# Decoder trunk, 288 tokens: norm sums as products with ones, pooling by doubling additions, first loads in pairs

## The chip, the cores and the metric

The kernel runs on one core of a Trainium2 chip. The metric is the device time of one execution in microseconds (us), the median of several runs, each against the same kernel before on the same chip. Less is better.

## The reference

One layer of a decoder trunk over 288 tokens: 256 of a new prompt and 8 x 4 new tokens of running requests, width 2048. All is float32. Cut to what matters:

```python
def trunk_layer(x, hist_conv, hist_pool, pos0, ...):
    h = rmsnorm(x, norm1_g)
    proj = einsum("btd,de->bte", h, w_in) + b_in          # 2048 -> 3 x 1024
    a, gate, z = proj[..., :1024], proj[..., 1024:2048], proj[..., 2048:]
    u_ext = concatenate([hist_conv, a * sigmoid(gate)], axis=1)
    c = silu(layernorm(depthwise_causal_conv(u_ext, conv_w, conv_b), ln_g, ln_b))   # 31 taps
    z_ext = concatenate([hist_pool, z], axis=1)
    d = multiscale_pool(z_ext, pos0)     # 4 groups of 256 channels: mean of the last 2, 4, 8, 16 tokens, minus z
    p = einsum("btgc,gce->btge", d, pool_w).reshape(bsz, T, 1024) * pool_scale
    x = x + einsum("btm,md->btd", concatenate([c, p], axis=-1), w_out)
    h2 = rmsnorm(x, norm2_g)
    x = x + einsum("btf,fd->btd", square(relu(einsum("btd,df->btf", h2, w_ff1))), w_ff2)   # 2048 -> 8192 -> 2048
```

A final rmsnorm follows, and the last conv and pool inputs are outputs as well. rmsnorm divides by the root of the mean square over the channels of a token (plus 1e-6); layernorm subtracts the mean first.

## The kernel before

**Layout.** Channels lie on the 128 partitions and the 288 tokens on the free axis, so xT is 128 x 16 x 288 in SBUF. A sum over the channels of a token thus runs across partitions, and TensorE has to do it.

**Products.** Float32 accuracy comes from three products in fp32r: a value is split in a high part (a cast on ScalarE) and a low part (value minus high part). `product` (L297) issues hi·hi (L300), hi·lo (L301) and lo·hi (L302), each 128x128 by 128x288. Weights are streamed by SP's queue into tiles `wr` (128x1024, six buffers) and split by `split` (L288) in `whi` on ScalarE (L293) and `wlo` on VectorE or GpSimd (L294), four buffers of each. An accumulator is a PSUM bank `ac` (four) or `cv` (two); two more banks `ms` hold sums.

**Stages**, in the order of the program:
1. A first loop over eight pairs of x blocks, c = 0 to 7 (L367-405), gives conv groups 0 and 1. For each block it makes hh and hl, x times the norm gain, split (L376, L377), and splits the weight (L383, L384). Steps c = 0 and 1 work on halves. `square(c)` (L357) squares the pair on ScalarE (128x576) and adds it up on VectorE; the 1/rms itself (`rb`, L404) is applied to the results of the products.
2. Conv groups 2 to 6, the pool groups 3, 2, 1, 0 and conv 7, in the order of SEQUENCE (L46), the pool mixes between. A conv group multiplies its two banks by rb (L416, L417), gates them, and runs 31 taps on VectorE and GpSimd (`conv_taps`, L443, L436).
3. w_out, pool half: 8 groups of 48 matmuls (L548-556). While they run, the conv layernorm is prepared: `norm_begin` (after the third group) subtracts the mean over channels and sums the squares in `ssc`, `norm_end` (after the fifth) forms the root and the eight pairs mh, ml of normed, SiLU'd channels.
4. w_out, conv half: 8 groups whose right-hand sides are those mh, ml (L560).
5. Four chunks of ff1 and ff2, and the final norm (L687).

**Sums before.** Per-token sums of squares come from `token_sum` (L232): three matmuls, with 96 tokens as the stationary operand and a column of ones, give 96x3 in PSUM. `rsqrt_rows` (L266) makes the reciprocal root of these 96x3 numbers: sqrt on ScalarE, then on VectorE one Newton-like step in five small instructions with two reciprocals (L275-279). Then three matmuls with an identity (L285, `pr`) spread them over all partitions as 128x288. For the conv norm's mean one float32 matmul with `avg` (ones/1024) is used (L521). Only the norm ahead of ff1 uses the wide way: `column_sum` (L244), two fp32r matmuls with a 128x128 of ones on the split squares, and `rsqrt_wide` (L249), the same step on 128x288.

**Pooling before.** `pool_group` (z with 15 tokens of history, L457-480) sums w = 2, 4, 8 or 16 neighbours by `tensor_reduce` on VectorE over overlapping windows; for w = 16 in two levels (L467-472).

**What sets the order.** The Tile scheduler puts all instructions in one order per engine, from the program's priorities and its own timeline. Each engine runs its row strictly in that order; a later instruction cannot pass a waiting one. The order below is that of the compiled program.

Of the kernel before, what the change touches and what calls it, by code (L numbers as in the profile page):

```python
# [88 lines left out]
def trunk_kernel(ctx: ExitStack, tc: tile.TileContext, io):  # L89
# [33 lines left out]
    def act(name, **kw):  # L123
        return slot(name, F32R, **(kw or {"tag": "act"}))
# [4 lines left out]
    def ms(name, n=512):  # L129
        return msp.tile([P, n], F32, name=nm(name), tag="ms", padded_shape=[P, 512])  # L130
# [7 lines left out]
    def f32(t):  # L138
        return t[:].bitcast(F32)
# [34 lines left out]
    def load_x(k, n):  # L174

        nc.sync.dma_start(xT[:, k : k + n, :], io["xT"][:, k : k + n, :])
# [6 lines left out]
        nc.sync.dma_start(to[:, :, k0:k1, :], src[:, :, at + k0 : at + k1, :])  # L183

    nc.scalar.dma_start(vec[:, 0:CWO], io["vec"][:, 0:CWO])
    load_x(0, 1)
    load_first(0, 0, 1)
    load_x(1, 1)
    load_first(0, 1, 2)
    load_x(2, 2)  # L190
    load_first(1, 0, 1)
    load_first(1, 1, 2)
    load_x(4, 2)
    load_first(2)
    load_x(6, 4)
    load_first(3)
    load_x(10, 4)
    load_first(4)
    load_x(14, 2)
    load_first(5)  # L200
    nc.sync.dma_start(vec[:, CWO:NV], io["vec"][:, CWO:NV])
    load_first(6)
# [2 lines left out]

    ones = const.tile([P, P], F32, name="ones")
    nc.vector.memset(ones, 1.0)
    avg = const.tile([P, P], F32, name="avg")
    nc.vector.memset(avg, 1.0 / DC)
    ones_r = const.tile([P, P], F32R, name="ones_r")  # L210
    nc.vector.memset(ones_r[:].bitcast(F32), 1.0)
    few = const.tile([P, 1], F32, name="few")
# [21 lines left out]
        for j in range(3):  # L234
            nc.tensor.matmul(pt[:TB, j : j + 1], t[:, j * TB : (j + 1) * TB], ones[:, 0:1], start=first and j == 0, stop=last and j == 2)  # L235

    def parts(t):

        th, tl = (tmpp.tile([P, T], F32R, name=nm(n), tag="tmp", bufs=6) for n in ("th", "tl"))
        nc.gpsimd.tensor_copy(th, t)  # L240
        nc.gpsimd.tensor_tensor(tl, t, f32(th), op=ALU.subtract)
        return th, tl

    def column_sum(bank, by, hilo):  # L244
# [1 line left out]
        for j, t in enumerate(hilo):  # L246
            nc.tensor.matmul(bank[:, :T], by, t, start=j == 0, stop=j == 1)

    def rsqrt_wide(bank, out, scale):  # L249

        s1, s2 = tmp("s"), tmp("s")
        b = bank[:, :T]
        nc.scalar.activation(s1, b, AF.Sqrt, bias=eps[:, 0:1], scale=scale)
        nc.vector.tensor_scalar(b, b, scale / 2, EPS / 2, op0=ALU.mult, op1=ALU.add)
        nc.vector.reciprocal(s2, s1)
        nc.vector.tensor_tensor(b, b, s2, op=ALU.mult)
        nc.vector.scalar_tensor_tensor(out=s2, in0=s1, scalar=0.5, in1=b, op0=ALU.mult, op1=ALU.add)
        nc.vector.reciprocal(out, s2)
# [93 lines left out]

    hx = []
    first_banks = bank2() + [bank("cv", cvp, "cv") for _ in range(2)]
    total = ms("total", 8)

    def square(c):  # L357

        to = squares[:, 0] if c == 0 else squares[:, 1 + c % 3]
        nc.scalar.activation(to, xT[:, 2 * c : 2 * c + 2, :], AF.Square)  # L360
# [6 lines left out]
    for c in range(8):  # L367
        pair = []
        hi = wspl.tile([P, 4, 256], F32R, name=nm("whi"), tag="whi")
        lo = wspl.tile([P, 4, 256], F32R, name=nm("wlo"), tag="wlo")  # L370
        views = [t[:].rearrange("p (b k) n -> p b k n", b=2) for t in (first_raw[c], hi, lo)]
        steps = ((0, 1), (1, 2)) if c < 2 else ((0, 2),)
        for k0, k1 in steps:
            for k in range(2 * c + k0, 2 * c + k1):
                hh, hl = act("hh"), act("hl")
                nc.scalar.activation(hh, xT[:, k, :], AF.Copy, scale=v("norm1_g", k))  # L376
                nc.vector.scalar_tensor_tensor(out=hl, in0=xT[:, k, :], scalar=v("norm1_g", k), in1=f32(hh), op0=ALU.mult, op1=ALU.subtract)  # L377
                pair.append((hh, hl))
            if len(steps) == 2:
                r, h, l = [t[:, :, k0, :] for t in views]  # L380
            else:
                r, h, l = first_raw[c], hi, lo
            nc.scalar.copy(h, r)  # L383
            nc.vector.tensor_tensor(l, r, h.bitcast(F32) if len(steps) == 2 else f32(hi), op=ALU.subtract)  # L384
            for w, x in ((hi, 0), (hi, 1), (lo, 0)):
                if c == 7 and w is lo:
                    token_sum(total, rows[0])
                for k in range(k0, k1):
                    for m in range(4):
                        nc.tensor.matmul(  # L390
                            first_banks[m][:, :T], lhs(w, k, m), pair[k][x],
                            start=c == 0 and k == 0 and w is hi and x == 0, stop=c == 7 and k == 1 and w is lo,
                        )
                if c == 7 and w is hi and x == 0:
                    square(6)
                    square(7)
                    rows = [row("tot")]
                    nc.vector.tensor_tensor(rows[0], squares[:, 0, 0], squares[:, 0, 1], op=ALU.add)
        hx += pair
        if 0 < c < 7:  # L400
            square(c - 1)
    ready.extend(itertools.islice(weights, 1))
    rb = row("rb")
    nc.vector.tensor_copy(rb, rsqrt_rows(total, 1.0 / D, AF.Sigmoid)[:, :T])  # L404
    nc.gpsimd.memset(z_all[:, :, 0:PH], 0.0)

    cs = {}
# [44 lines left out]
    def pool_group(g):  # L452

        bk = bank2()
        gemm(bk, hx)
        w = WINDOWS[g]
        for m in range(2):  # L457
            i = 2 * g + m
            z = z_all[:, i, :]
            zs = samples(z[:, ZO:ZL], ZS)  # L460
            p = tmp("p")
            nc.vector.tensor_tensor(p, bk[m][:, :T], rb, op=ALU.mult)
            nc.scalar.activation(z[:, PH:ZO], p[:, 0:SEQ], AF.Identity, bias=v("b_in", 16 + i))
            nc.scalar.activation(zs[:, :, PH:ZS], samples(p[:, SEQ:T], NS), AF.Identity, bias=v("b_in", 16 + i))
            b = ms("d")[:, :T]
            s, step, n = z, 1, w
            if w > 8:  # L467
                s, step, n = tmp("s", ZL, "s", 2), 4, w // 4
                nc.vector.tensor_reduce(s[:, 3:ZL], windows(z[:, 0 : ZL - 3], (1, ZL - 3), (1, 4)), axis=AX.X, op=ALU.add)
            at = PH - step * (n - 1)  # L470
            nc.vector.tensor_reduce(b[:, 0:SEQ], windows(s[:, at:], (1, SEQ), (step, n)), axis=AX.X, op=ALU.add)
            nc.vector.tensor_reduce(samples(b[:, SEQ:T], NS), windows(s[:, ZO + at :], (ZS, NB), (1, NS), (step, n)), axis=AX.X, op=ALU.add)
            nc.vector.tensor_tensor(b[:, 0 : w - 1], b[:, 0 : w - 1], rise[:, g, 0 : w - 1], op=ALU.mult)
            nc.vector.scalar_tensor_tensor(out=b[:, 0:SEQ], in0=b[:, 0:SEQ], scalar=1.0 / w, in1=z[:, PH:ZO], op0=ALU.mult, op1=ALU.subtract)
            bs = samples(b[:, SEQ:T], NS)
            nc.vector.scalar_tensor_tensor(out=bs, in0=bs, scalar=1.0 / w, in1=zs[:, :, PH:], op0=ALU.mult, op1=ALU.subtract)
# [41 lines left out]
    def norm_begin():  # L518

        pmean = ms("pmean")  # L520
        nc.tensor.matmul(pmean[:, :T], avg, sum_c, start=True, stop=True)  # L521
        ssc = row("ssc")
        for i in range(N8):
            nc.vector.tensor_tensor(cs[i], cs[i], pmean[:, :T], op=ALU.subtract)
            if i == 0:
                nc.scalar.activation(ssc, cs[i], AF.Square)
            else:
                q = bank("q", cvp, "cv")[:, :T]
                nc.scalar.activation(q, cs[i], AF.Square)
                nc.vector.tensor_tensor(ssc, ssc, q, op=ALU.add)  # L530
        return ssc

    def norm_end(ssc):

        pt = ms("pt", 8)
        token_sum(pt, ssc)
        rl = rsqrt_rows(pt, 1.0 / DC, AF.Silu)
        for i in range(N8):
            n = tmp("n")
            nc.vector.tensor_tensor(n, cs[i], rl[:, :T], op=ALU.mult)  # L540
            mh, ml = act("mh"), act("ml")
            cc = tmp("cc") if i < N8 - 1 else uz[:, N8 * UL - T - 120 : N8 * UL - 120]
            nc.scalar.activation(cc, n, AF.Silu, bias=v("ln_b", i), scale=v("ln_g", i))
            nc.scalar.copy(mh, cc)
            nc.vector.tensor_tensor(ml, cc, f32(mh), op=ALU.subtract)
            mixc.append((mh, ml))
# [214 lines left out]
```

## Time and profile before

| | us |
|---|---|
| median of 3 runs (1076.07 to 1076.46) | 1076.26 |
| the profiled execution's own time | 1076.56 |
| its span (first to last instruction) | 1074.7 |
| TensorE busy | 1062.6 |
| VectorE busy | 942.6 |
| GpSimd busy | 752.3 |
| ScalarE busy | 478.8 |

Of the profile's rows: `start, duration, engine, line, operation, out<-in, xcount`, and in brackets the engine's idle time just ahead and what ended it. PE is TensorE, DVE VectorE, ACT ScalarE, POOL GpSimd, SP the engine that issues most loads. Rows of a grouped view end in `busy us, mean ns | idle`. In rows of windows: the stretch, its length, and for each engine the busy time and count; then the mean granted TensorE clock, the share and the rate of the DMA engines. L numbers before are those of the kernel above. A matmul's row shows its whole flight; the step from one start to the next is what it costs in a stream.

### The profile page before, as it was taken

The page shows a single profiled execution, that of the slowest core. Times are in us where ns is not written, and L with a number is a line of the kernel's source. Part 1 is how long each engine was busy: PE and PEld are TensorE (multiplying, and loading weights), DVE is VectorE, ACT ScalarE, POOL GpSimd, SP SyncE. Part 2 cuts the span into 40 slices and gives each one's busy share as a digit, 9 for nine tenths or more (in the row PEclk, how much of TensorE's full clock was granted, in tenths as well). Part 3 has the DMA queues.
Part 4 walks back from the last instruction along what each step waited for, and adds up shares of the span by engine and source line. Part 5 has one row for each costly group of instructions (what it writes and reads, how often), then busy time and mean ns, then how long its engine had stood idle before and what let it go on. Part 6 is the DMA issues. An engine that isn't in the chain of part 4 may idle for free.

```text
span 1074.7 us, 21425 instructions
## 1 busy us (share of the span) xinstructions
PE 1062.6 (99%) x8163; PEld 1061.3 (99%) x8163; DVE 942.6 (88%) x2117; ACT 478.8 (45%) x650; POOL 752.3 (70%) x400
## 2 busy tenths in 40 slices
PE   8999999999999999999999999999999999999996
PEld 8999999999999999999999999999999999999996
DVE  7799999687399999999999999999999999999553
ACT  7544455576445433334444333444433334444441
POOL 0899888503889987788888877888878788850001
PEclk9999999999999999999999999999999999999998
DMA  9655567565687777777797777777778888885522
GB/s 334 225 187 177 179 192 216 173 200 165 216 287 249 259 250 250 250 248 251 239 276 247 251 246 250 247 253 248 242 241 281 277 268 270 276 260 174 170 97 89
DMA packets 74663, 247.38 MB, mean 230 GB/s; under 512 B 7872, under 2 KB 17088, under 8 KB 74560
## 3 DMA queue, kind: packets, MB, share of 16 engines
q1 hardware_dynamic: 74128, 245.36, 70.0%
q8 instruction: 64, 1.05, 0.4%
q10 hardware_dynamic: 432, 0.64, 0.2%
q14 instruction: 39, 0.32, 0.1%
HBM read 241.25 MB, written 4.72 MB: 229 GB/s over the span
## 4 chain that ended last, share of the span: by engine, by line
PE 98%; DMA 0%; DVE 0%; ACT 0%; SPq 0%; issue 0%; DVEq 0%
PE ac L300 32%; PE ac L301 32%; PE ac L302 32%; PE ac L390 1%; PE cv L390 1%; DMA xT<-in_xT 0%; DVE xT L693 0%; PE pr L285 0%; ACT hh L376 0%; ACT uz L360 0%; PE pf L235 0%; ACT whi L383 0%; PE m L300 0%; PE m L302 0%; PE m L301 0%
## 5 line engine op out<-in xcount | busy, mean ns | idle before, releaser
L294 POOL TENSOR_TENSOR wlo<-wr,whi 128x1024 fp32r<-128x1024 f32 x282 | 675.7, 2404 | 177.9 <-ACT whi L293 177.1
L621 DVE SCALAR_TENSOR_TENSOR own<-uz,own 128x288 f32<-128x288 f32 x1397 | 605.1, 519 | 0.0
L293 ACT CAST whi<-wr 128x1024 fp32r<-128x1024 f32 x330 | 345.2, 1047 | 537.0 <-PE ac L301 485.1
L302 PE MATMUL ac<-ah,wlo 128*128 128x288 f32 x1024 | 298.1, 291 | 0.0
L301 PE MATMUL ac<-al,whi 128*128 128x288 f32 x1024 | 298.1, 291 | 0.0
L300 PE MATMUL ac<-ah,whi 128*128 128x288 f32 x1024 | 298.1, 291 | 0.0
L300 PE MATMUL ac<-fh,whi 128*128 128x288 f32 x1013 | 295.0, 291 | 0.0
L302 PE MATMUL ac<-fh,wlo 128*128 128x288 f32 x1013 | 294.9, 291 | 0.0
L301 PE MATMUL ac<-fl,whi 128*128 128x288 f32 x1013 | 294.9, 291 | 0.0
L302 PEld LDWEIGHTS ac<-ah,wlo 128*128 128x128 f32 x1024 | 191.7, 187 | 0.0
L300 PEld LDWEIGHTS ac<-ah,whi 128*128 128x128 f32 x1024 | 191.7, 187 | 0.0
L301 PEld LDWEIGHTS ac<-al,whi 128*128 128x128 f32 x1024 | 191.7, 187 | 0.0
L300 PEld LDWEIGHTS ac<-fh,whi 128*128 128x128 f32 x1013 | 189.6, 187 | 0.0
L301 PEld LDWEIGHTS ac<-fl,whi 128*128 128x128 f32 x1013 | 189.6, 187 | 0.0
L302 PEld LDWEIGHTS ac<-fh,wlo 128*128 128x128 f32 x1013 | 189.6, 187 | 0.0
L443 DVE SCALAR_TENSOR_TENSOR pc<-uz,vec,pc 128x256 f32<-128x256 f32 x232 | 99.2, 485 | 5.3 <-ACT pc L432 3.5
L301 PE MATMUL ac<-hl,whi 128*128 128x288 f32 x320 | 92.1, 291 | 0.0
L300 PE MATMUL ac<-hh,whi 128*128 128x288 f32 x320 | 92.0, 291 | 0.0
L302 PE MATMUL ac<-hh,wlo 128*128 128x288 f32 x320 | 87.3, 291 | 0.0
L294 DVE TENSOR_TENSOR wlo<-wr,whi 128x1024 fp32r<-128x1024 f32 x48 | 58.7, 1224 | 29.9 <-ACT whi L293 29.8
L693 POOL TENSOR_TENSOR xT<-xT,rg 128x576 f32<-128x576 f32 x2 | 2.8, 1408 | 99.4 <-ACT rg L698 99.4
L648 POOL TENSOR_TENSOR fl<-f,fh 128x288 fp32r<-128x288 f32 x64 | 53.5, 836 | 15.3 <-ACT fh L647 15.3
(174 smaller groups left out, 1056.0 us busy)
## 6 DMA issues: line engine op xcount, KB each, us to landing
wr<-in_w SPq DMA_DIRECT2D x336, 512.0 KB, 4.6
uz<-fd SPq DMA_DIRECT2D x96, 576.0 KB, 5.8
uz<-in_w SPq DMA_DIRECT2D x24, 128.0 KB, 6.8
out_u_out<-uz SPq DMA_DIRECT2D x1, 1208.0 KB, 8.8
xT<-in_xT SPq DMA_DIRECT2D x2, 576.0 KB, 8.1
uz<-in_hist_c SPq DMA_DIRECT2D x1, 1088.0 KB, 12.0
wr<-in_w SPq DMA_DIRECT2D x4, 256.0 KB, 5.4
xT<-in_xT SPq DMA_DIRECT2D x3, 288.0 KB, 6.1
```

Of the source, the lines that this page charges most:

```text
L293: nc.scalar.copy(hi[:, a:b, :], raw[:, a:b, :])
L294: eng.tensor_tensor(lo[:, a:b, :], raw[:, a:b, :], hi[:, a:b, :].bitcast(F32), op=ALU.subtract)
L300: nc.tensor.matmul(b, wh, xh, start=first, stop=False)
L301: nc.tensor.matmul(b, wh, xl, start=False, stop=False)
L302: nc.tensor.matmul(b, wl, xh, start=False, stop=last)
L390: nc.tensor.matmul(first_banks[m][:, :T], lhs(w, k, m), pair[k][x], start=c == 0 and k == 0 and w is hi and x == 0, stop=c == 7 and k == 1 ...
L443: nc.vector.scalar_tensor_tensor(out=dst, in0=u_all[:, i, w : w + SEQ], scalar=cw[i][:, w : w + 1], in1=pc[i], op0=ALU.mult, op1=ALU.add)
L621: nc.vector.scalar_tensor_tensor(out=to, in0=at[:, r, :], scalar=by, in1=to, op0=ALU.mult, op1=ALU.add)
L648: nc.gpsimd.tensor_tensor(fl, f, f32(fh), op=ALU.subtract)
L693: eng.tensor_tensor(xk, xk, by[:, None, :T].to_broadcast([P, n, T]), op=ALU.mult)
```

## The change

Five edits:
- `token_sum` and `rsqrt_rows` are no longer used for the token norm (`total`) and the conv norm (`pt`): both are now `column_sum` on a split pair th, tl and `rsqrt_wide`. The mean (`pmean`) is a `column_sum` as well, its 1/1024 applied by a VectorE instruction (`scalar_tensor_tensor` with -1/DC). `avg` is gone.
- `parts` makes its pair on ScalarE (high) and VectorE (low) instead of on GpSimd, except for the norm ahead of ff1.
- `pool_group` copies (ScalarE) and adds (VectorE) at doubling steps 1, 2, 4, 8 over all of the row, where it reduced over windows.
- The first x loads are of two blocks; the high halves of both blocks come first on ScalarE, then the low ones. The four first squares are written over raw weight tiles that are used up, and square(0), (1), (2) are put later (after steps 2 and 3).
- A PAD tile `gap` is cleared on GpSimd at the start.

The diff, cut:

```diff
-    load_x(0, 1)
+    load_x(0, 2)
     load_first(0, 0, 1)
-    load_x(1, 1)
     load_first(0, 1, 2)
...
-    load_x(6, 4)
+    load_x(6, 2)
     load_first(3)
-    load_x(10, 4)
+    load_x(8, 4)
     load_first(4)
-    load_x(14, 2)
+    load_x(12, 4)
...
-    def parts(t):
+    def parts(t, hi=nc.scalar.copy, lo=nc.vector):
...
-        nc.gpsimd.tensor_copy(th, t)
-        nc.gpsimd.tensor_tensor(tl, t, f32(th), op=ALU.subtract)
+        hi(th, t)
+        lo.tensor_tensor(tl, t, f32(th), op=ALU.subtract)
...
-    def rsqrt_wide(bank, out, scale):
+    def rsqrt_wide(bank, out, scale, after=None):
...
+        if after is not None:
+            load_table(after, s1[:, 0:1])
...
-        to = squares[:, 0] if c == 0 else squares[:, 1 + c % 3]
+        to = squares[:, 1 + c % 3]
+        if c < 4:
+            to = first_raw[2 + c % 2][:].rearrange("p a b -> p (a b)")[:, 0 : 2 * T].rearrange("p (k t) -> p k t", t=T)
...
-                    token_sum(total, rows[0])
+                    column_sum(total, ones_r, hilo)
...
-        if 0 < c < 7:
+        if c == 2:
+            first_square = square(0)
+        elif c == 3:
+            square(1)
+            square(2)
+        elif 3 < c < 7:
             square(c - 1)
     ready.extend(itertools.islice(weights, 1))
     rb = row("rb")
-    nc.vector.tensor_copy(rb, rsqrt_rows(total, 1.0 / D, AF.Sigmoid)[:, :T])
+    rsqrt_wide(total, rb, 1.0 / D, AF.Sigmoid)
...
-            s, step, n = z, 1, w
-            if w > 8:
-                s, step, n = tmp("s", ZL, "s", 2), 4, w // 4
-                nc.vector.tensor_reduce(s[:, 3:ZL], windows(z[:, 0 : ZL - 3], (1, ZL - 3), (1, 4)), axis=AX.X, op=ALU.add)
...
+            s, r = ms("d"), z
+            for step in WINDOWS[: g + 1]:
+                n = ZL - step + 1
+                nc.scalar.copy(s[:, 0:n], r[:, 0:n])
+                to = s if step == w else tmp("r", ZL, "r", 2)
+                nc.vector.tensor_tensor(to[:, 0:n], s[:, 0:n], r[:, step // 2 : step // 2 + n], op=ALU.add)
+                r = to
...
-        nc.tensor.matmul(pmean[:, :T], avg, sum_c, start=True, stop=True)
+        column_sum(pmean, ones_r, parts(sum_c))
...
-        pt = ms("pt", 8)
-        token_sum(pt, ssc)
-        rl = rsqrt_rows(pt, 1.0 / DC, AF.Silu)
+        rl = ms("pt")
+        column_sum(rl, ones_r, parts(ssc))
+        rsqrt_wide(rl, rl[:, :T], 1.0 / DC, AF.Silu)
```

The order of instructions moves with it. First VectorE at the end of the pool half of w_out, before, from the root's first step (pt, st) to the first normed channel block (n), with wlo of weight block 68 and the two additions of a w_out group into xT between:

```order
L275 TENSOR_SCALAR pt_2661<-pt_2661 96x3
L276 RECIPROCAL st_2665<-st_2665 96x3
L277 TENSOR_TENSOR pt_2661<-pt_2661,st_2665 96x3
L552 TENSOR_TENSOR xT<-xT,ac_2804 128x288
L278 SCALAR_TENSOR_TENSOR st_2665<-st_2665,pt_2661 96x3
L552 TENSOR_TENSOR xT<-xT,ac_2805 128x288
L279 RECIPROCAL st_2665<-st_2665 96x3
L294 TENSOR_TENSOR wlo_2927<-wr_2920,whi_2926 128x1024
L540 TENSOR_TENSOR n_2677<-c_540,pr_2673 128x288
```

The same stretch of VectorE after the change; ac_2903 and ac_2904 are the banks of the last pool-half group, and wlo_3022 and wlo_3026 two weight blocks of the conv half:

```order
L257 TENSOR_SCALAR pt_2696<-pt_2696 128x288
L258 RECIPROCAL s_2704<-s_2703 128x288
L297 TENSOR_TENSOR wlo_3022<-wr_3017,whi_3021 128x1024
L259 TENSOR_TENSOR pt_2696<-pt_2696,s_2704 128x288
L568 TENSOR_TENSOR xT<-xT,ac_2903 128x288
L568 TENSOR_TENSOR xT<-xT,ac_2904 128x288
L260 SCALAR_TENSOR_TENSOR s_2704<-s_2703,pt_2696 128x288
L297 TENSOR_TENSOR wlo_3026<-wr_3019,whi_3025 128x1024
L261 RECIPROCAL pt_2696<-s_2704 128x288
L556 TENSOR_TENSOR n_2712<-c_538,pt_2696 128x288
```

The small steps on 96x3 have become steps on 128x288, and the additions that stand between the two reciprocals are no longer those of an earlier group but those of the last one (before, they stood behind the first n).

TensorE at the seam of the two halves, after the change: the last rows of the pool half (ac_2904, right-hand sides ph, pl) and the first of the conv half (mh_2714 is made from the n above):

```order
L303 MATMUL ac_2904<-ph_2332,whi_2893 128x288
L304 MATMUL ac_2904<-pl_2333,whi_2893 128x288
L305 MATMUL ac_2904<-ph_2332,wlo_2894 128x288
L303 MATMUL ac_2967<-mh_2714,whi_2957 128x288
L303 MATMUL ac_2968<-mh_2714,whi_2957 128x288
L303 MATMUL ac_3043<-mh_2714,whi_3021 128x288
L303 MATMUL ac_3044<-mh_2714,whi_3021 128x288
L304 MATMUL ac_2967<-ml_2715,whi_2957 128x288
```

Nothing stands on TensorE between the last pool-half matmul and the first on mh. The sum pt's second matmul, which was 58 rows ahead of this seam before (its three matmuls end there), stands 32 rows ahead of it now.

ScalarE at the start, before: hh are high halves of x blocks, whi of the first weights (halves, 128x2x256, for steps c = 0 and 1), the rows with uz the squares:

```order
L376 ACTIVATE hh_178<-xT,vec 128x288
L383 CAST whi_176<-wr_90 128x2x256
L376 ACTIVATE hh_196<-xT,vec 128x288
L360 ACTIVATE uz<-xT 128x576
L383 CAST whi_176<-wr_90 128x2x256
L376 ACTIVATE hh_216<-xT,vec 128x288
L360 ACTIVATE uz<-xT 128x576
L376 ACTIVATE hh_234<-xT,vec 128x288
L383 CAST whi_214<-wr_91 128x2x256 x2
```

And after the change:

```order
L384 ACTIVATE hh_177<-xT,vec 128x288
L384 ACTIVATE hh_195<-xT,vec 128x288
L392 CAST whi_175<-wr_92 128x2x256 x2
L384 ACTIVATE hh_215<-xT,vec 128x288
L384 ACTIVATE hh_233<-xT,vec 128x288
L392 CAST whi_213<-wr_93 128x2x256 x2
L384 ACTIVATE hh_253<-xT,vec 128x288
L384 ACTIVATE hh_254<-xT,vec 128x288
L392 CAST whi_251<-wr_94 128x1024
```

The squares have left this stretch; the first of them now stands behind the cast of step c = 3.

More of the change, by code (lines that the diff above doesn't have):

```diff
@@ L40 @@
 ZL = ZO + NB * ZS
+PAD = 32
 LATER = 1000000
@@ L152, in trunk_kernel @@
     squares = uz[:, N8 * UL : N8 * UL + 8 * T].rearrange("p (n k t) -> p n k t", k=2, t=T)
+    gap = const.tile([P, PAD], F32, name="gap")
+    nc.gpsimd.memset(gap, 0.0)
     def v(key, j):
@@ L207, in trunk_kernel @@
     nc.vector.memset(ones, 1.0)
-    avg = const.tile([P, P], F32, name="avg")
-    nc.vector.memset(avg, 1.0 / DC)
     ones_r = const.tile([P, P], F32R, name="ones_r")
@@ L354, in trunk_kernel @@
     first_banks = bank2() + [bank("cv", cvp, "cv") for _ in range(2)]
-    total = ms("total", 8)
+    total = ms("total")
     def square(c):
-        to = squares[:, 0] if c == 0 else squares[:, 1 + c % 3]
+        to = squares[:, 1 + c % 3]
+        if c < 4:
+            to = first_raw[2 + c % 2][:].rearrange("p a b -> p (a b)")[:, 0 : 2 * T].rearrange("p (k t) -> p k t", t=T)
         nc.scalar.activation(to, xT[:, 2 * c : 2 * c + 2, :], AF.Square)
         if c:
-            nc.vector.tensor_tensor(squares[:, 0], squares[:, 0], to, op=ALU.add)
+            nc.vector.tensor_tensor(squares[:, 0], first_square if c == 1 else squares[:, 0], to, op=ALU.add)
+        return to
     def lhs(t, k, m):
@@ L373, in trunk_kernel @@
         for k0, k1 in steps:
-            for k in range(2 * c + k0, 2 * c + k1):
-                hh, hl = act("hh"), act("hl")
+            his = [act("hh") for _ in range(k0, k1)]
+            los = [act("hl") for _ in range(k0, k1)]
+            blocks = range(2 * c + k0, 2 * c + k1)
+            for k, hh in zip(blocks, his):
                 nc.scalar.activation(hh, xT[:, k, :], AF.Copy, scale=v("norm1_g", k))
+            for k, hh, hl in zip(blocks, his, los):
                 nc.vector.scalar_tensor_tensor(out=hl, in0=xT[:, k, :], scalar=v("norm1_g", k), in1=f32(hh), op0=ALU.mult, op1=ALU.subtract)
-                pair.append((hh, hl))
+            pair += zip(his, los)
             if len(steps) == 2:
@@ L398, in trunk_kernel @@
                     nc.vector.tensor_tensor(rows[0], squares[:, 0, 0], squares[:, 0, 1], op=ALU.add)
+                    hilo = parts(rows[0])
         hx += pair
-        if 0 < c < 7:
+        if c == 2:
[4 more added lines that the diff above has]
+        elif 3 < c < 7:
             square(c - 1)
@@ L464, in pool_group @@
             nc.scalar.activation(zs[:, :, PH:ZS], samples(p[:, SEQ:T], NS), AF.Identity, bias=v("b_in", 16 + i))
-            b = ms("d")[:, :T]
-            s, step, n = z, 1, w
-            if w > 8:
-                s, step, n = tmp("s", ZL, "s", 2), 4, w // 4
[L469 to L476, printed above, removed]
+            s, r = ms("d"), z
[5 more added lines that the diff above has]
+                r = to
+            at = PH - (w - 1)
+            b, bp = s[:, 0:T], s[:, at : at + SEQ]
+            nc.vector.tensor_tensor(bp[:, 0 : w - 1], bp[:, 0 : w - 1], rise[:, g, 0 : w - 1], op=ALU.mult)
+            nc.vector.scalar_tensor_tensor(out=b[:, 0:SEQ], in0=bp, scalar=1.0 / w, in1=z[:, PH:ZO], op0=ALU.mult, op1=ALU.subtract)
+            ends = windows(s[:, ZO + at :], (ZS, NB), (1, NS))
+            nc.vector.scalar_tensor_tensor(out=samples(b[:, SEQ:T], NS), in0=ends, scalar=1.0 / w, in1=zs[:, :, PH:], op0=ALU.mult, op1=ALU.subtract)
             dh, dl = act("dh", tag="p", bufs=16), act("dl", tag="p", bufs=16)
@@ L520, in norm_begin @@
         pmean = ms("pmean")
-        nc.tensor.matmul(pmean[:, :T], avg, sum_c, start=True, stop=True)
+        column_sum(pmean, ones_r, parts(sum_c))
         ssc = row("ssc")
         for i in range(N8):
-            nc.vector.tensor_tensor(cs[i], cs[i], pmean[:, :T], op=ALU.subtract)
+            nc.vector.scalar_tensor_tensor(out=cs[i], in0=pmean[:, :T], scalar=-1.0 / DC, in1=cs[i], op0=ALU.mult, op1=ALU.add)
             if i == 0:
@@ L626, in trunk_kernel @@
     r2 = row("r2")
-    ss2 = parts(ss2)
+    ss2 = parts(ss2, nc.gpsimd.tensor_copy, nc.gpsimd)
     turn(0)
```

## The prediction

> **What bounds the kernel now.** I read the page first: span, busy shares, and the engines in the chain that ended last.
>
> ```profile
> span 1074.7 us, 21425 instructions
> PE 1062.6 (99%) x8163; PEld 1061.3 (99%) x8163; DVE 942.6 (88%) x2117; ACT 478.8 (45%) x650; POOL 752.3 (70%) x400
> PE 98%; DMA 0%; DVE 0%; ACT 0%; SPq 0%; issue 0%; DVEq 0%
> ```
>
> TensorE is busy for 99% of the span, and it is 98% of the chain that ended last. The other engines have slack on average. So a microsecond of matmul that goes is a microsecond gained, and any wait that TensorE gains is added in full. VectorE time that goes is worth nothing unless TensorE waits for it. The view of TensorE's waits says how little it waits now:
>
> ```profile
> PE ac L390 <- ACT whi L383: 1.7, 1, 1.7
> PE pr L285 <- DVE st L279: 0.5, 1, 0.5
> ```
>
> One wait of 1.7 us lies in the first loop, and one of 0.5 us after the last matmul of the feed-forward part. I looked next, in the timeline, at the place where the pool half of w_out meets its conv half, because the second norm must be ready there:
>
> ```profile
> 215.70 0.29 PE L300 MATMUL ac<-ph,whi 128*128 128x288 f32 x1
> 215.83 0.29 PE L301 MATMUL ac<-pl,whi 128*128 128x288 f32 x1
> 215.96 0.29 PE L302 MATMUL ac<-ph,wlo 128*128 128x288 f32 x1
> 216.09 0.42 PE L300 MATMUL ac<-mh,whi 128*128 128x288 f32 x2
> ```
>
> Starts are 0.13 us apart across that seam: a 128x288 matmul costs 0.13 us, and TensorE waits for nothing there. I call the end of the last pool-half matmul G (about 216.25).
>
> **The change part by part.**
>
> *Sums on TensorE.* The chain of waits has what goes:
>
> ```profile
> 27.70 0.43 PE total L235 x6
> 32.92 0.64 PE pr L285 x6
> 196.75 0.48 PE pmean L521 x2
> 207.63 0.43 PE pt L235 x6
> 212.60 0.64 PE pr L285 x6
> ```
>
> Together 0.43 + 0.64 + 0.48 + 0.43 + 0.64 = 2.62 us. In their place stand three sums of two matmuls 128x288: 6 x 0.13 = 0.78 us. The difference is **-1.84 us**, certain, since all of it is on TensorE.
>
> *The conv norm's root.* Before, the statistics lie as 96x3, so each VectorE step takes about 0.17 us:
>
> ```profile
> 208.37 1.28 ACT L218 ACT_TABLE_LOAD   x1
> 209.80 0.17 DVE L279 RECIPROCAL st<-st 96x3 f32<-96x3 f32 x1
> 210.84 1.23 DVE L294 TENSOR_TENSOR wlo<-wr,whi 128x1024 fp32r<-128x1024 f32 x1 [0.87 <-ACT whi L293]
> 213.28 0.46 DVE L540 TENSOR_TENSOR n<-c,pr 128x288 f32<-128x288 f32 x1 [1.21 <-PE pr L285]
> 213.77 0.63 ACT L543 ACTIVATE cc<-n,vec 128x288 f32<-128x288 f32 x1 [0.30 <-DVE n L540]
> 214.43 0.43 ACT L544 CAST mh<-cc 128x288 fp32r<-128x288 f32 x1
> ```
>
> mh was ready at 214.86, 1.4 us before G. Now the statistics are 128x288, as in the norm ahead of the feed-forward part, whose rows give the prices:
>
> ```profile
> 278.10 0.50 ACT L253 ACTIVATE s<-pss,eps 128x288 f32<-128x288 f32 x1
> 278.64 0.47 DVE L254 TENSOR_SCALAR pss<-pss 128x288 f32<-128x288 f32 x1 [3.05 <-ACT s L253]
> 279.01 1.94 DVE L255 RECIPROCAL s<-s 128x288 f32<-128x288 f32 x1
> 280.99 0.47 DVE L256 TENSOR_TENSOR pss<-pss,s 128x288 f32<-128x288 f32 x1
> 281.49 0.45 DVE L257 SCALAR_TENSOR_TENSOR s<-s,pss 128x288 f32<-128x288 f32 x1
> 281.98 1.95 DVE L258 RECIPROCAL r<-s 128x288 f32<-128x288 f32 x1
> ```
>
> A reciprocal is 12 times what it was. The start is later too: the second matmul of the sum stands 32 matmuls ahead of the end of the last pool group, so it ends about G - 4.1 (before, the sum ended at G - 8.2). From the order of instructions: root on ScalarE to G - 3.5, then its table load (1.28) and a tiny activation, then whi (1.05) to G - 1.1. VectorE: scale to G - 3.1, reciprocal to G - 1.1, a wlo (1.23) to G + 0.2, product to G + 0.6, two xT additions at 0.4 each, which need the group's end, to G + 1.4, the fused step to G + 1.8, **another wlo to G + 3.0**, second reciprocal to G + 4.9, n to G + 5.4. ScalarE: cc (0.63), a second cc (about 0.55) ahead of mh, then mh (0.43): G + 7.0. Issues that overlap by 0.1 us each (279.01 starts before 278.64 + 0.47 is over) take up to 0.7 off. TensorE has nothing else in its order, since the next row is the first matmul on mh. I take **+6.6 us**, bounds 5.5 and 7.5. After that each mh feeds twelve matmuls (1.56 us) and follows the last within 1.0 us on ScalarE, so no further wait.
>
> *The clock.* [...] The windows of the tail show what it does:
>
> ```profile
> 1062.00:1066.00 4.00, 3.33 (x28) 2.90 (x27) 1.30 (x8) 1.24 (x3) 0.00 (x0) 1.00 0.00 0
> 1066.00:1070.00 4.00, 0.09 (x1) 0.00 (x0) 3.53 (x5) 0.40 (x1) 2.77 (x2) 0.91 0.78 298
> 1070.00:1074.00 4.00, 0.00 (x0) 0.00 (x0) 0.00 (x0) 0.00 (x0) 0.00 (x0) 0.50 0.73 292
> ```
>
> The last matmul ended at 1066.09. A mean of 0.91 over 4 us between 1.0 and 0.5 puts the drop at 1069.3, or 3.2 us of idleness. A stall of 6.6 us is twice that. Getting back up is seen at the start:
>
> ```profile
> 1.05 3.82 PE L223 MATMUL warm<-ones 128*128 128x128 f32 x18 [1.05 <-DVE ones L207]
> 3.77 1.10 PE L223 MATMUL warm<-ones 128*128 128x128 f32 x6
> ```
>
> The first 12 warm passes took 2.72 us (0.23 each), the last six 1.10 (0.18 with the drain), so speed rose some 3 us after the first. Three us at half speed lose 1.5: I take **+1.5 us**, bounds 0 and 1.7.
>
> [...]
>
> *First loads and squares.* ScalarE and the first matmul of the loop's second step (c = 1), from the timeline, before:
>
> ```profile
> 7.10 0.67 ACT L360 ACTIVATE uz<-xT 128x576 f32<-128x576 f32 x1
> 8.18 0.53 ACT L376 ACTIVATE hh<-xT,vec 128x288 fp32r<-128x288 f32 x1
> 9.62 1.13 ACT L383 CAST whi<-wr 128x512 fp32r<-128x512 f32 x2
> 10.28 0.53 PE L390 MATMUL ac<-hh,whi 128*128 128x288 f32 x2
> ```
>
> ScalarE sets when that step can start (10.28): it worked without a gap from 7.10, with a square (0.57 from start to start) at 7.10 and one more between the hh at 8.18 and the casts at 9.62. The data of that hh, xT 2-3, had landed by 8.18. With the squares put behind, two hh (0.43 each at this pitch) and one half cast (0.52) bring the step to about 9.6, 0.7 earlier, if xT 2-3 lands as before. But the squares must still run before the loop's end, ahead of the casts of the fifth to seventh steps, and xT 4-5, 6-7 and 8-11 now come just as ScalarE wants them. I take **0** for the loop, bounds -1.8 (the wait of 1.7 named above goes, and the step comes early) and +1.0 (two square pairs show in full). Squares in raw tiles delay two later weight loads, but those queue on SP behind hist_c in any case.
>
> *The token root ahead of the convs.* VectorE's last product on the first two banks and its first taps, before:
>
> ```profile
> 35.19 0.46 DVE L417 TENSOR_TENSOR ac<-ac,rb 128x288 f32<-128x288 f32 x1
> 38.27 4.06 DVE L443 SCALAR_TENSOR_TENSOR pc<-uz,vec,pc 128x256 f32<-128x256 f32 x10 [1.53 <-POOL wlo L294]
> ```
>
> The sum now stands inside conv group 2, and the wide chain (278.64 to 283.93 above, 5.3 us) delays the gates by 7 to 9 us: the taps start near 45, and the two banks come free about when group 3 wants them (45.8, the end of group 2 at 0.13 us a matmul). I take **+0.2**, bounds 0 and 1.0.
>
> *Pooling.* By form, over the conv and w_out stage:
>
> ```profile
> L471 DVE TENSOR_REDUCE d<-uz 128x256 f32<-128x2048 f32 x2 | 4.6, 2310 | 0.0
> L469 DVE TENSOR_REDUCE s<-uz 128x420 f32<-128x1680 f32 x2 | 3.8, 1894 | 0.0
> L471 DVE TENSOR_REDUCE d<-s 128x256 f32<-128x1024 f32 x2 | 3.8, 1888 | 0.0
> ```
>
> 4.6 + 3.8 + 3.8 = 12.2 us go in these three, and the reductions of the shorter windows besides. Added are 2 x (1+2+3+4) = 20 additions of about 128x415, between 0.46 (128x288, above) and 1.23 (the wlo of 128x1024): nearer the first, 0.5, so 10 us, and 20 copies on ScalarE of about 0.5. VectorE saves a few us, but TensorE did not wait for VectorE here, so this gives nothing. The mixes move a little and the chain ScalarE copy, VectorE add is longer, so a bank or cast may be late at the last mix: **+0.3**, bounds 0 and 2.0.
>
> **Sum**, against the profiled execution's 1076.56 (0.3 above the median of the three runs): -1.84 + 6.6 + 1.5 + 0 + 0.2 + 0.3 = +6.8, **1083.3 us**.
>
> **The rivals.**
> 1. *The pause is there, the clock holds.* [...] Then 1081.8. Or the pause is short of 3.2, because wlo moves or n comes early; nothing in the order does that.
> 2. *No pause: the seam stays covered.* For it: 1.4 us of slack stood there, and the sum could be done sooner if the ssc additions end early. Against it: VectorE's row order puts the second reciprocal behind two additions that need the group's end, so even instant arithmetic ends after G. Then only -1.84 and perhaps the loop's gain: 1073.5 to 1075, **faster**. It decides if the conv norm's chain from sum to mh takes under 4.1 us; its two reciprocals alone are 3.9.
> 3. *More late banks or casts.* The bounds of group 3, the mix seam and the first loop come together: +2.5 more, 1086.
> 4. *The change's gains at the front are whole* and the pause is there: 1081.5.
>
> **How the numbers follow.** The forecast with its neighbours (1082.3 to 1085) gets 0.53; rival 1, 0.13; rival 4, 0.09; rival 3, 0.09; rival 2, 0.10; the rest, a pause cut to 1 to 3 us by orders I mis-timed (1076 to 1079), 0.06. The range holds 1077.5 to 1086.5. About 0.2% (2.2 us) is what a measurement of this kernel tells from no change: faster by more 0.06, within 0.09, slower by more 0.85.
>
> **What would show it.** In the profile after: TensorE's waits should name ScalarE's mh for 5.5 to 7.5 us, once; the slice of the granted clock near 220 should dip; the chain should hold two wide reciprocals of 1.95 us near 213 and 221 and no row with pr there; the pool rows should be additions of about 0.55. I am wrong if TensorE's starts run on 0.13 us apart across G, or if the wait there is under 3 us.

## The result and the profile after

The changed kernel takes **1084.67 us** (median of 4 runs, 1084.36 to 1084.87) against 1076.16 for the kernel before: 8.5 us more, a ratio of 1.0079 with a 95% interval of 1.0061 to 1.0096. The profiled execution took 1084.69, 8.13 us more than that of before. Its page:

```profile
span 1082.9 us, 21396 instructions
PE 1064.5 (98%) x8143; PEld 1061.9 (98%) x8143; DVE 951.1 (88%) x2120; ACT 488.6 (45%) x673; POOL 753.5 (70%) x401
PE 95%; ACT 1%; DMA 1%; DVE 1%; issue 0%; SPq 0%; POOL 0%; DVEq 0%; POOLq 0%; ACTq 0%
```

TensorE is still the chain, but three points of it have gone to other engines. The view of TensorE's waits says where:

```profile
PE ac L303 <- ACT mh L560: 6.6, 1, 6.6
PE ac L399 <- ACT whi L392: 0.9, 2, 0.5
PE ac L303 <- ACT tg L433: 0.2, 1, 0.2
PE ac L305 <- POOL wlo L297: 0.2, 1, 0.2
```

One wait of 6.6 us for mh is new, and the 1.7 us in the first loop has become 0.9. TensorE's timeline at the seam between the pool half and the conv half of w_out:

```profile
215.12 0.29 PE L304 MATMUL ac<-pl,whi 128*128 128x288 f32 x1
215.25 0.29 PE L305 MATMUL ac<-ph,wlo 128*128 128x288 f32 x1
222.13 1.33 PE L303 MATMUL ac<-mh,whi 128*128 128x288 f32 x4 [6.59 <-ACT mh L560]
223.26 0.44 PE L304 MATMUL ac<-ml,whi 128*128 128x288 f32 x1
223.50 0.44 PE L305 MATMUL ac<-mh,wlo 128*128 128x288 f32 x1
```

The step from 215.25 to 222.13 is 6.88 us where 0.13 was due: a pause of 6.75 us. And behind it the starts are 0.24 us apart, not 0.13. The windows show why:

```profile
218.00:220.00 2.00, 0.00 (x0) 0.00 (x0) 2.00 (x2) 0.00 (x0) 0.00 (x0) 1.00 0.48 152
220.00:222.00 2.00, 0.00 (x0) 0.00 (x0) 1.69 (x5) 1.39 (x4) 0.00 (x0) 0.53 0.46 178
...
224.00:226.00 2.00, 2.00 (x10) 2.00 (x10) 1.94 (x5) 2.00 (x6) 0.00 (x0) 0.50 0.00 0
226.00:228.00 2.00, 2.00 (x14) 2.00 (x13) 1.26 (x4) 1.52 (x5) 0.00 (x0) 0.76 0.00 0
```

The granted clock (the last figure but two) fell at 220.1 (0.53 over 2 us is 0.12 us at full speed) and came back at 227.0. VectorE's timeline is the row that set the pause:

```profile
212.33 1.94 DVE L258 RECIPROCAL s<-s 128x288 f32<-128x288 f32 x1
214.40 1.23 DVE L297 TENSOR_TENSOR wlo<-wr,whi 128x1024 fp32r<-128x1024 f32 x1
215.54 0.46 DVE L259 TENSOR_TENSOR pt<-pt,s 128x288 f32<-128x288 f32 x1
215.91 0.81 DVE L568 TENSOR_TENSOR xT<-xT,ac 128x288 f32<-128x288 f32 x2
216.64 0.45 DVE L260 SCALAR_TENSOR_TENSOR s<-s,pt 128x288 f32<-128x288 f32 x1
217.00 1.22 DVE L297 TENSOR_TENSOR wlo<-wr,whi 128x1024 fp32r<-128x1024 f32 x1
218.14 1.95 DVE L261 RECIPROCAL pt<-s 128x288 f32<-128x288 f32 x1
220.12 1.60 DVE L556 TENSOR_TENSOR n<-c,pt 128x288 f32<-128x288 f32 x4
```

Nearly all of it lies behind the pool half's last matmul, and mh came at 222.08.

**Where the 8.13 us are.** Matmuls of the sums -1.84; pause +6.75; half clock +2.2 (the conv half's first matmul stands 6.04 later than before, its last one 8.24 later); waits ahead of the seam +1.3, between 34 and 171 us (0.27 at the token sum, the others for tg, wlo and mixes). Together these are 8.4; the 0.3 too much lies in no one place. The first loop ends where it did: its last matmul starts at 32.70 against 32.63, with four matmuls of the next group ahead of it (0.52 us), where before the token sum stood (0.43).

### The profile page after: what moved, and what is told of

It reads as the page before. It is cut to its first block, busy times and chain, and to the rows that moved or that the text cites. A ratio compares the mean times of both kernels' runs of the same rounds, so it can differ in the third digit from the quotient of the medians.

```text
span 1082.9 us, 21396 instructions
## 1 busy us (share of the span) xinstructions
PE 1064.5 (98%) x8143; PEld 1061.9 (98%) x8143; DVE 951.1 (88%) x2120; ACT 488.6 (45%) x673; POOL 753.5 (70%) x401
## 4 chain that ended last, share of the span: by engine, by line
PE 95%; ACT 1%; DMA 1%; DVE 1%; issue 0%; SPq 0%; POOL 0%; DVEq 0%; POOLq 0%; ACTq 0%
PE ac L303 31%; PE ac L305 31%; PE ac L304 31%; DMA wr<-in_w 1%; PE ac L399 0%; PE cv L399 0%; DVE xT L709 0%; DMA vec<-in_vec 0%; ACT whi L392 0%; ACT hh L384 0%; DVE wlo L297 0%; ACT wr L365 0%; ACT whi L296 0%; DVE pt L261 0%; ACT uz L365 0%
```

## The experiments

All medians, each beside runs of the kernel before on the same chip (1076.27 to 1076.44 in the three sets). The changed kernel was measured beside 1076.16, so a difference to it is good to some 0.3 us.

**1. The conv norm's root narrow again.**

```diff
-        rl = ms("pt")
-        column_sum(rl, ones_r, parts(ssc))
-        rsqrt_wide(rl, rl[:, :T], 1.0 / DC, AF.Silu)
+        pt = ms("pt", 8)
+        token_sum(pt, ssc)
+        rl = rsqrt_rows(pt, 1.0 / DC, AF.Silu)
```

> The changed kernel with the conv norm's sum and root put back to 96x3 (three matmuls for the sum, three to spread it). Theory (the wide root makes the pause, and the pause halves the clock): the pause of 6.75 us and the 2.2 us of half clock go, 0.81 us of matmul comes back (0.43 + 0.64 - 0.26), and since the spreading matmuls stand 8 rows ahead of the seam (1.04 us) and mh needs 1.7 us after them, about 0.7 us of pause stays: 1084.67 - 8.95 + 0.81 + 0.7 = 1077.2 us. Rival (the time comes from the late taps or the pooling, and TensorE only happens to wait for mh): the pause stays above 3 us and the time above 1081.

Measured: 1080.40 us (ratio 1.0038, 1.0023 to 1.0053). In the profiled execution the clock stayed at 1.0 at the seam, and the waits there are

```profile
PE ac L303 <- ACT mh L560: 1.5, 1, 1.5
PE ac L304 <- DVE ml L561: 0.9, 1, 0.9
```

So the wide root accounts for 4.3 of the 8.5 us in this kernel, not for nearly all: 3 us more stayed than was expected. The narrow sum here stands at 209.8, not at 207.8 as before, and ScalarE put a weight cast between cc and mh. Something ahead of the norm was late as well.

**2. Keep TensorE busy in the pause.**

```diff
+    idle = ms("idle")
+    for _ in range(26):
+        nc.tensor.matmul(idle[:, 0:P], ones, xT[:, 14, 0:P], start=True, stop=True)
```

> The changed kernel with 26 plain matmuls 128x128 whose result is not used, put on TensorE between the pool half's last matmul and the first on mh (they wait for the last block but one of xT, about 0.6 us into the pause, and take 5.5 us). Theory (the 2.2 us after the pause are half clock, brought by idleness): the granted clock stays at 1.0 through the seam, the matmuls after it are 0.13 us apart, and the time falls by 2.2 to 1082.5 us, with mh still late. Rival (after the pause TensorE is slow because mh and ml come one by one): no change, 1084.7.

Measured: 1082.69 us, 2.0 less than the changed kernel. TensorE's timeline of it:

```profile
216.61 6.07 PE L576 MATMUL idle<-xT,ones 128*128 128x128 f32 x52 [0.87 <-DVE xT L568]
222.44 0.77 PE L303 MATMUL ac<-mh,whi 128*128 128x288 f32 x4
223.05 0.29 PE L304 MATMUL ac<-ml,whi 128*128 128x288 f32 x1
223.18 0.29 PE L305 MATMUL ac<-mh,wlo 128*128 128x288 f32 x1
```

The trace shows the 26 float32 matmuls as 52. mh is as late as it was, but the granted clock is 1.00 in every window from 214 to 228, and the matmuls behind the pause are 0.13 apart, where the changed kernel with its idle TensorE had 0.50 and 0.24. In this case the slow stretch was the clock, and it went when TensorE was not idle.

**3. The two wlo out of the root's way.**

```diff
-        for _ in range(8):
-            yield halves([split(raw, V) for raw in load()])
+        for j in range(8):
+            yield halves([split(raw, G if j < 2 else V) for raw in load()])
```

> The changed kernel with the low halves of the first two groups of the conv half made on GpSimd instead of VectorE. In VectorE's order the two wlo then no longer stand between the root's steps, the second reciprocal stands ahead of the last group's two additions, and the sum ends 0.8 us earlier. Theory (the pause is the root's two reciprocals plus what stands between them): mh at G + 3.5 rather than 6.75. With the clock halved after it 1081.4 us, without 1079.2; the pause is close to the 3.2 us at which the clock fell in the tail. Rival (the two reciprocals and the late start are all of it): the pause stays above 5.5 and the time above 1083.

Measured: 1081.93 us, a pause of 3.7. Its windows:

```profile
216.00:218.00 2.00, 0.00 (x0) 0.00 (x0) 2.00 (x6) 0.91 (x2) 1.49 (x2) 0.96 0.36 113
222.00:224.00 2.00, 2.00 (x10) 2.00 (x10) 1.51 (x4) 2.00 (x6) 0.00 (x0) 0.50 0.05 16
224.00:226.00 2.00, 2.00 (x15) 2.00 (x14) 0.83 (x2) 0.57 (x2) 0.00 (x0) 0.84 0.00 0
```

The pause shrank by 3.0 us, as the sum of durations on VectorE said. The time fell by 2.7 only, since the clock fell again, at 217.8, and came back at 224.6: 5.5 us of the half clock lay behind the restart (at 219.18), where it was 4.8.

**4. The wide conv norm alone, on the kernel before.**

> The kernel before with the wide sum and root of the conv norm alone. Theory (that one edit carries the loss): the sum's second matmul stands 50 rows ahead of the seam (6.6 us), three wlo and both additions lie between it and the first n, mh about 5 us after the seam, the clock halves: 1076.16 + 5 + 2.2 - 0.8 = 1082.6 us. Rival (the loss needs the other edits, which make everything ahead late): the chain fits, and the time is 1075.4 to 1077.

Measured: 1083.00 us (ratio 1.0063, 1.0046 to 1.0079), with a pause of 5.5 and half clock after it (0.50 in the windows from 220 to 224). One edit is enough for 6.6 of the 8.5 us.

**5. Pooling by reductions again.** In the changed kernel the body of `pool_group` goes back to `tensor_reduce` over windows.

> The changed kernel with the pooling put back to reductions over windows. Theory (what the additions save on VectorE is spent ahead of the seam: the wide token root starts the taps some 7 us later, and the shorter pooling just makes that up): in the compiled order the mean of the conv channels falls back by 72 matmuls (9 us) and the sum of squares to the last two places ahead of the seam, so the pause grows from 6.75 to about 11 us; 1084.67 + 4.5 = 1089 us. Rival, as the prediction had it (VectorE's saving is worth nothing, as TensorE does not wait for VectorE there): 1084.7 within 1.

Measured: 1090.52 us, 5.9 more than the changed kernel. TensorE's timeline:

```profile
214.55 0.29 PE L305 MATMUL ac<-ph,wlo 128*128 128x288 f32 x1
219.05 0.61 PE L248 MATMUL pt<-th,ones_r 128*128 128x288 f32 x1 [4.21 <-ACT th L241]
219.54 0.61 PE L248 MATMUL pt<-tl,ones_r 128*128 128x288 f32 x1
228.06 1.33 PE L303 MATMUL ac<-mh,whi 128*128 128x288 f32 x4 [7.91 <-ACT mh L559]
```

Now TensorE waits for the sum of squares too, and the way from the last pool-half product to the first on mh is 13.4 us too long, where 11 was expected. The shorter pooling was worth 5.9 us inside this change, although no wait of TensorE in the pooling stage is put down to VectorE.

**6. The mean by one float32 matmul again.**

```diff
-        column_sum(pmean, ones_r, parts(sum_c))
+        nc.tensor.matmul(pmean[:, :T], avg, sum_c, start=True, stop=True)
...
-            nc.vector.scalar_tensor_tensor(out=cs[i], in0=pmean[:, :T], scalar=-1.0 / DC, in1=cs[i], op0=ALU.mult, op1=ALU.add)
+            nc.vector.tensor_tensor(cs[i], cs[i], pmean[:, :T], op=ALU.subtract)
```

> The changed kernel with the conv channels' mean put back to one float32 matmul (0.48 us, no split of sum_c). In the profile after, the split's low half on VectorE took 2.18 us where the same form took 0.45 elsewhere; it ended when GpSimd's wlo did. Theory (that instruction, with two inputs in SBUF, is held up by GpSimd, and the split with it delays the mean by about 2 us): the mean stands 1.5 to 2 us earlier, the pause falls by about 1.5 to 5.3 us, TensorE pays 0.22 more, 1083.4 us. Rival (the pause hangs on the order behind the sum alone): 1084.9.

Measured: 1083.67 us; the pause fell to 5.9 (5.3 was expected), the mean came 1.3 us earlier (196.9 for 198.2). The row it rested on, in the changed kernel:

```profile
194.85 2.18 DVE L242 TENSOR_TENSOR tl<-sum_c,th 128x288 fp32r<-128x288 f32 x1 [1.46 <-ACT th L241]
```

**7. A wide root that starts early.** On the kernel before: pooling by additions, wide conv norm, and the edit of experiment 3.

> The kernel before with three things: the pooling by doubling additions, the wide sum and root of the conv norm, and the low halves of the first two groups of the conv half on GpSimd. Token sum, mean and first loads are those of before. Theory (a wide root costs nothing where it starts early enough): the taps start at 38 as before and the pooling is shorter, so the mean stands 26 matmuls earlier than before and the sum ends about 9 us ahead of the seam; the chain needs 7; no pause, and 0.81 us of matmul is saved: 1075.4 us. Rival (the wide root on VectorE always comes late at this seam): a pause of more than 2 us, above 1077.5.

Measured: 1076.98 us (ratio 1.0005, 0.9996 to 1.0014). From the timelines of TensorE, VectorE and GpSimd, in this order:

```profile
214.72 0.29 PE L308 MATMUL ac<-ph,wlo 128*128 128x288 f32 x1
214.85 1.10 PE L306 MATMUL ac<-mh,whi 128*128 128x288 f32 x4
```

```profile
215.78 0.45 DVE L552 TENSOR_TENSOR ml<-cc,mh 128x288 fp32r<-128x288 f32 x1
...
216.85 1.95 DVE L552 TENSOR_TENSOR ml<-cc,mh 128x288 fp32r<-128x288 f32 x1
```

```profile
216.04 2.44 POOL L300 TENSOR_TENSOR wlo<-wr,whi 128x1024 fp32r<-128x1024 f32 x1 [0.67 <-ACT whi L299]
```

The seam has no pause: 214.72 to 214.85 is one step, 1.24 us earlier than before. The same wide root costs TensorE nothing at the seam here. But then TensorE lost 1.9 us in three pieces, and the expected gain was gone. The two larger ones, 0.6 and 0.9, were waits for ml; the first was not, as it stands among the matmuls on mh.

**8. Wide token root and additions, on the kernel before.**

> The kernel before with the pooling by additions and the wide token sum and root alone (conv norm, mean and first loads as before). Theory (the wide token root costs late taps, which the shorter pooling pays back): the conv norm's sums stand where they stood before, no pause at the seam, 0.81 us of matmul saved, 0.1 to 0.4 us lost around the sum: 1075.6 us. Rival (late taps cost TensorE time by themselves, at the mixes or the banks): 1077 or more.

Measured: 1077.59 us (ratio 1.0010, 1.0001 to 1.0019): a miss of 2 us, on the rival's side. There was no pause at the seam, and at 195.8 the mean stood 1 us earlier than before. But TensorE waited 0.7 us for a weight cast near 86 us and 1.0 for ml after the seam, neither of which is at the rival's mixes. Why that cast was late was not followed up. The taps started at 40.8, 2.5 us later than before.

**9. The waits for ml in 7 taken out.** As 7, with the last of the four wlo back on VectorE, and in the first two groups of the conv half another order of the three products (cut):

```diff
         nc.tensor.matmul(b, wh, xh, start=first, stop=False)
+        if lo_last:
+            nc.tensor.matmul(b, wl, xh, start=False, stop=False)
+            nc.tensor.matmul(b, wh, xl, start=False, stop=last)
+            return
```

> As e7_pool_wide_end_wlo, with two things more: the last of the four low halves goes back to VectorE, and in the first two groups of the conv half each product takes mh by whi and wlo first and ml by whi last. In e7 there was no pause at the seam, but TensorE then waited 1.9 us in three pieces for ml, one of which VectorE wrote in 1.95 us while GpSimd was at a wlo. Theory (the two-input VectorE instruction is held up by GpSimd): without a wlo on GpSimd after 215, ml takes 0.45, TensorE waits 0.7 in all, and the time is 1075.7 us. Rival (ml is late for the order on VectorE alone): 1076.5 or more.

Measured: 1075.64 us (ratio 0.9995, 0.9986 to 1.0003). The second ml now took 0.46 us:

```profile
217.87 0.46 DVE L556 TENSOR_TENSOR ml<-cc,mh 128x288 fp32r<-128x288 f32 x1
```

That is 9.0 us below the changed kernel with the wide root kept. Below the kernel before it is 0.6, which its interval doesn't separate from none. What each of the two edits gave is not separated.

**10. First loads and moved squares alone, on the kernel before.**

> The kernel before with the first loads in pairs and the moved squares alone. Theory (later squares make the token sum late, so the taps start later, and without the shorter pooling the conv norm comes late at the seam, though its root is the narrow one): in the compiled order the mean is 27 matmuls later than before, the spreading matmuls stand right at the seam, and the pause is about 4 us with half clock after it: 1082 us. Rival (the first loop ends at the same time, so that nothing follows): 1076.4.

Measured: 1083.60 us (ratio 1.0070, 1.0054 to 1.0085). The first loop ends when it did, and yet:

```profile
PE ac L305 <- ACT mh L560: 3.3, 1, 3.3
PE pr L290 <- DVE st L284: 1.4, 2, 0.9
```

These are TensorE's waits. The 3.3 and one 0.9 lie at the same seam, with the *narrow* root (the other 0.5 is that of the final norm, as before): the taps started at 42.4 instead of 38.3, the sum of squares stood at 214.6 instead of 207.8.

**11. Pooling by additions alone, on the kernel before.**

> The kernel before with the pooling by additions alone. Theory (it brings the conv norm forward, where nothing waits for it): the mean stands 26 matmuls earlier than before (3.4 us), TensorE runs on without a pause as it did before: 1076.2 us, no difference that can be measured. Rival (the longer chain of copies and additions makes mixes late): 1077 or more.

Measured: 1076.28 us (ratio 0.9999, 0.9990 to 1.0008). The mean came 3.5 us earlier (193.3 for 196.8), and nothing waited for it.

**12. The changed kernel with the old first loads and squares.**

> The changed kernel with the first loads and the squares put back. Theory (the front gains and loses nothing within the change, and the pause hangs on the conv norm's chain): the order at the seam is the same to 3 matmuls, the pause stays 6.5 to 7, the time 1084.3 within 0.7. Rival (the stalls between 141 and 170 us, 1.0 us in all, come from the front): 1083.3 and those stalls gone.

Measured: 1083.54 us, 1.1 less than the changed kernel, just under the theory's range and near the rival's time. The pause is the same 6.75, and the clock is low for the same 6.8 us (218.44 to 225.28 by the windows):

```profile
221.61 1.33 PE L304 MATMUL ac<-mh,whi 128*128 128x288 f32 x4 [6.59 <-ACT mh L550]
```

```profile
218.00:220.00 2.00, 0.00 (x0) 0.00 (x0) 1.97 (x3) 0.00 (x0) 0.00 (x0) 0.61 0.64 193
...
224.00:226.00 2.00, 2.00 (x13) 2.00 (x13) 1.62 (x5) 2.00 (x6) 0.00 (x0) 0.68 0.00 0
```

But only 3.7 us of the half clock lie behind the restart, where it was 4.8: that is 0.5 of the 1.1 us. The other 0.5 lies ahead of the seam (last pool-half matmul at 214.73 instead of 215.25). The waits of 0.36 and 0.31 us near 163 and 170 are gone, as the rival had it, and one of 0.7 near 86 is new, as in experiment 8.

**The chain that joins them.** Starts in the timelines (us): VectorE's first taps, the last matmul of the mean and of the sum of squares, then mh's end, and TensorE's pause at the seam.

| kernel | taps | mean | sum | mh ready | pause |
|---|---|---|---|---|---|
| before | 38.3 | 196.8 | 207.8 | 214.9 | 0 |
| 11, additions alone | 38.1 | 193.3 | 204.8 | 211.3 | 0 |
| 7, additions, early wide root | 38.0 | 193.2 | 205.6 | 214.8 | 0 |
| 4, wide conv norm alone | 37.8 | 196.4 | 208.1 | 220.2 | 5.5 |
| 10, first loads and squares alone | 42.4 | 200.3 | 214.6 | 220.7 | 5.3 (1.1 of it ahead of the spreading matmuls, which take part of the rest) |
| 1, changed, narrow conv norm | 46.4 | 198.8 | 209.8 | 218.5 | 1.7 |
| changed | 45.9 | 198.2 | 211.1 | 222.1 | 6.8 |
| 12, changed, old first loads and squares | 41.6 | 197.4 | 210.6 | 221.6 | 6.8 |
| 5, changed, old pooling | 45.7 | 207.1 | 219.5 | 228.0 | 13.4 (the sum's two matmuls in it) |

Long pooling, a wide root and, in experiment 10, a late front all push on one date, mh at the seam. Before, 1.2 us was left there (mh ready at 214.86, used at 216.09), and an edit that pushes beyond it makes a pause. The edit that pulls (the additions) costs and gives nothing alone, and 5.9 us among the others. The pushes don't simply add up: in experiment 12 the taps start 4.3 us earlier than in the changed kernel, yet mean, sum and mh come only 0.5 to 0.8 earlier, the seam itself comes 0.5 earlier, and the pause is the same. What takes up the rest between taps and mean was not followed up.

## Why the prediction was right, and where its terms were off

Forecast 1083.3 in a range of 1077.5 to 1086.5; measured 1084.67. Between the profiled executions, +6.8 was forecast and +8.1 measured.

- **Pause at the seam**, forecast +6.6 by adding up VectorE's and ScalarE's rows in their new order: 6.75 measured. Experiments 1, 3 and 4 changed parts of that sum, and the pause went the way the durations said, to within 0.3 us in 3 and 0.5 in 4; in 1 it was 1.7 instead of 0.7, since ScalarE's extra cast had been left out.
- **The clock**, forecast +1.5 with an upper bound of 1.7, which no run shows: it was 2.2, outside it. The drop was foreseen from the tail, but its length was taken from the start-up's 3 us. The clock was at half for 6.8 us (220.12 to 226.96), of which 4.8 lay behind the restart: 20 matmuls at 0.24 instead of 0.13. Experiment 2 took 2.0 of it away. This is the term that was mis-sized. The half clock was as long, 6.8 us, in experiments 3 and 12, but 5.5 and 3.7 us of it lay behind the restart; in 12, with the same pause, about 1.7 us were lost, an estimate from 15 matmuls at 0.24 instead of 0.13. What sets that share no run shows.
- **Sums on TensorE**, -1.84: two matmuls at the common pitch stand for each. No run contradicts it, none isolates it.
- **First loop**, forecast 0: 0 within 0.1, by the starts of its last matmul. TensorE's first product starts later (5.73 for 4.81) and waits less. But a forecast for the loop missed what follows from it. With the moved squares the token sum stands later, at 32.7 instead of 27.5 us in experiment 10, and alone that edit costs 7.3 us (6.4 in the profiled execution, with a pause of 5.3 at the seam). Inside the change it costs at most 1.1 us, and no pause (experiment 12). What hides it there, the additions or the late token root, no run separates.
- **Token root**, +0.2: the wait at the sum is 0.27, and taps at 45 were forecast, 45.9 measured. The banks were in time. The lateness has two sources that were taken as one: the wide token root with the old first loads starts the taps at 40.8 to 41.6 (experiments 8 and 12), and the new first loads and squares add 4.3. Part of it was not seen at all: two instructions of the sum, tot and tl, took 2.53 and 2.08 us instead of 0.45 each, beside a `wlo` on GpSimd, as shown below.
- **Pooling**: forecast 0 on the ground that TensorE does not wait for VectorE in that stage. Each addition took 0.59 us (0.5 was forecast), so VectorE saves a little less. But the reason failed: experiment 5 shows 5.9 us behind it. The slack of an engine in one stage is a date in a later one. The small waits at the mixes were forecast at 0.3 and are 1.0; they don't come from the additions alone, as experiments 11 and 12 have the same additions and none of these waits.
- **Rival 2** (no pause) named the right condition, a chain from sum to mh that ends ahead of the seam because the sum is done sooner; experiments 7 and 9 are that case. The changed kernel was not, by 7 us.

## What to carry to other kernels

When one engine is the bound, don't ask what the others' work costs, but when its results are due: follow each edit to the next place where the bound engine needs them, and keep the margin there as a number (1.2 us here). Replacing small VectorE steps on 96x3 by steps on 128x288 saves matmuls but multiplies a reciprocal's time by 12 (0.16 to 1.94 us); it is free only where that date has room (experiment 9), and no run here shows a gain from it that is clear of the noise. And a pause of the matrix engine can be dearer than its length (2.2 us on top of 6.75 here): price the clock with it.

## What the runs showed of the hardware

**Four VectorE instructions with two inputs in SBUF took 1.95 to 2.53 us instead of 0.45 beside a `wlo` on GpSimd.** The token sum's addition, in VectorE's timeline of the changed kernel with a reciprocal for comparison, then GpSimd's timeline of the same kernel, then VectorE's of the kernel before:

```profile
29.92 2.53 DVE L407 TENSOR_TENSOR tot<-uz 128x288 f32<-128x288 f32 x1
...
36.42 1.94 DVE L258 RECIPROCAL s<-s 128x288 f32<-128x288 f32 x1
```

```profile
28.73 5.98 POOL L297 TENSOR_TENSOR wlo<-wr,whi 128x1024 fp32r<-128x1024 f32 x2 [26.36 <-ACT whi L296]
...
34.80 4.83 POOL L297 TENSOR_TENSOR wlo<-wr,whi 128x1024 fp32r<-128x1024 f32 x2
```

```profile
24.27 0.45 DVE L398 TENSOR_TENSOR tot<-uz 128x288 f32<-128x288 f32 x1
```

2.53 us for what took 0.45 when GpSimd had not begun. The split of the mean (2.18) and ml in experiment 7 (1.95) did the same, and experiment 9, with GpSimd idle there, gave ml in 0.46. Each ended 0.3 us after the wlo that GpSimd was at: 197.03 after 196.72 for the mean, 218.80 after 218.48 for ml. Four additions with one input in PSUM (ssc, between 204.1 and 206.2) took 0.45 each beside a wlo that lasted from 203.83 to 206.24. The reciprocal, with one input, took 1.94 beside a busy GpSimd and 1.94 beside an idle one (212.33). One row does not fit: in the changed kernel the addition of the squares at 29.14, with two inputs in SBUF, took its usual 0.75 although the `wlo` on GpSimd is recorded from 28.73; that `wlo` lasted 3.41 us, where the mean is 2.41. Why, no run shows. The prediction priced tl and tot without the added time.

**The half clock lasted 3.4, 6.8 or 13.7 us, and began 2.2 to 4.6 us after the last matmul.** By the windows it lasted 6.8 us in the changed kernel and in experiments 3, 4, 6 and 12 (mean clock of each profiled execution 0.994), and 13.7 in experiment 5 (218.7 to 232.3; mean clock 0.991). It began 4.6 us after the last matmul's end in the changed kernel, 2.2 in experiment 3 and 3.2 in the tail. In experiment 10 it lasted 3.4 us only (mean clock 0.995):

```profile
220.00:222.00 2.00, 1.29 (x5) 1.29 (x6) 1.55 (x4) 2.00 (x6) 0.00 (x0) 0.57 0.65 240
222.00:224.00 2.00, 2.00 (x12) 2.00 (x10) 1.92 (x6) 2.00 (x7) 0.00 (x0) 0.57 0.00 0
```

(from 220.3 to 223.7). A pause of 1.7 us (experiment 1) left the clock at 1.0 in the profiled execution; two of its four runs have a mean clock of 0.995 instead of 0.997, so there it may have fallen.
